# A decoder layer on one core: the feed-forward products cut into 2x2 blocks, seven block products in place of eight

## The chip, the core and the metric

The kernel runs on one core of a Trainium2 chip. A core has a tensor engine (PE in the profile; PEld is its loading of weights), a vector engine (DVE), a scalar engine (ACT), a GpSimd engine (POOL) and a queue that issues most of the transfers (SP). Each engine works through its own queue in order, and waits on semaphores for the others. All data that an engine computes on lies in the on-chip memory of 128 partitions; the tensor engine writes into eight accumulator banks. The metric is the device time of one execution in microseconds (us).

## The reference, cut to what matters

1032 tokens (1024 of a prompt, 8 samples) with 1024 channels go through one decoder layer. In front of the change stand a norm, an input projection, sliding-window attention, a diagonal state-space branch (S5) and a gated merge. The change concerns what follows:

```python
x = x + merged @ w_out                        # 1024 -> 1024
h2 = rms_norm(x, norm2_g)
x = x + (silu(h2 @ w_ffn_gate) * (h2 @ w_ffn_up)) @ w_ffn_down   # 1024 -> 2816 -> 1024
y = rms_norm(x, norm_f_g)
```

with `rms_norm(x, g) = x * rsqrt(mean(x * x) + 1e-5) * g`, all in float32.

## The kernel before

Activations are stored with channels on the 128 partitions and tokens along the free axis: eight tiles of 128 x 1032 make up x. A matrix product goes by output tiles of 128 channels, three chunks of 344 tokens each (`CH`, `NCH`), and input tiles of 128 channels. Float32 is kept by a split: an operand v is written as a high part (v rounded to a shorter format, by ACT) and a low part (v minus the high part, by DVE), and each product is three matmuls: high x high, high x low and low x high (`mm3`, L118 to L120). So one output tile of the gate matrix (`fg`) takes 8 x 3 x 3 = 72 matmuls of 344 columns.

`load_w` brings a weight tile of 128 x 512 from memory (`wr`), splits it (L107 on ACT, L108 on DVE) into `wh` and `wl`, three buffers each, and hands out blocks of 128 columns.

The order of the work that the change touches:

- Output projection (`wo`): for eight output tiles, three chunks; the residual is added (L1001), the result (`mg`, the new x) is multiplied by norm2_g and split (`hh` on ACT L1002, `hl` on DVE L1003), and its squares are summed (`s2`). The norm's factor of each token, `r2`, is ready later; it isn't applied to x but to the products behind it.
- Feed-forward (FFN): 22 output tiles of gate and up, in four parts of 6, 6, 6 and 4 (`FSPLIT`). For each tile: gate product (`fg`), times r2 (L1052), sigmoid (ACT L1053), times itself, times r2 (L1055, L1056); up product (`fu`), times that (L1062), and the result is split into `idh`, `idl`, which stay on chip. After each part its share of the down product (`fd`) is added to x (L1072). The last part runs by blocks of 384, 384 and 264 tokens, and the final norm and the output follow block by block (L1082, L1084, L1141).

The whole body is handed to a scheduler, which puts each engine's instructions in an order of its own before they are placed in the queues; a tile that shares a buffer (tag) with another waits until that one's last reader is done.

## Time and profile before

| | |
|---|---|
| three timed runs | 1456.91 us median (1455.76 to 1459.46) |
| profiled execution, first to last instruction (span) | 1455.0 us |
| PE busy | 1404.8 us (97%) |
| DVE, ACT, POOL busy | 800.7, 458.9, 193.5 us |

The profile gives no other time of the profiled execution than its span, which lies 1.9 us under the median of the timed runs. The stages, read from the tensor engine's timeline: input projection, attention, S5 and merge until 598.3 us; output projection until about 689.5; FFN until 1440.9; norm and output until 1455. A matmul's length in the rows is longer than the time to the next one, since they are pipelined: rates are read from the starts. "idle before ... <-" names what ended an engine's wait.

### The profile page before, as it was taken

Reading aid. Unit: us, or ns where it says so; the run is one execution under the profiler, and the core shown is the slowest. Engines: PE = TensorE matmul, PEld = TensorE weight load, DVE = VectorE, ACT = ScalarE, POOL = GpSimd, SP = SyncE. Lnnn points to the kernel's source line nnn. Section 1 sums busy time; section 2 is a strip of 40 time slices with the busy share of each in tenths; the row PEclk is TensorE's granted clock in tenths of the full one; section 3 lists DMA queues with packets and bytes.
Section 4 is the critical chain, followed back from the end, with each engine's and each line's share of the span. In section 5 each row is a group of like instructions: output and inputs, shape, how many; then the busy total and the mean of one; then the engine's idle time right before and its main releaser. Section 6 shows DMA issues by size and latency. Waiting matters only on the chain.

```text
span 1455.0 us, 22291 instructions
## 1 busy us (share of the span) xinstructions
PE 1404.8 (97%) x8839; PEld 1370.5 (94%) x8839; DVE 800.7 (55%) x1825; ACT 458.9 (32%) x967; POOL 193.5 (13%) x218
## 2 busy tenths in 40 slices
PE   7799999998899999999999999999999999999996
PEld 6689999997788999999999999999999999999996
DVE  4675976269988744655744423444334444335447
ACT  3323655433334623333322211222111222113242
POOL 1113321066673001000000000000000000000004
PEclk9799999999999999999999999999999999999998
DMA  6111100111111111223111111111111111123003
GB/s 230 50 36 61 30 16 16 44 60 46 31 32 39 59 54 31 77 88 96 47 49 44 35 53 58 45 44 40 45 50 56 44 44 45 48 63 94 29 1 117
DMA packets 52393, 78.02 MB, mean 54 GB/s; under 512 B 12090, under 2 KB 24386, under 8 KB 52289
## 3 DMA queue, kind: packets, MB, share of 16 engines
q1 hardware_dynamic: 50960, 73.79, 16.5%
q0 software_dynamic: 640, 2.10, 0.5%
q8 instruction: 69, 1.13, 0.3%
q10 hardware_dynamic: 688, 0.72, 0.1%
q14 instruction: 36, 0.29, 0.1%
HBM read 69.84 MB, written 5.55 MB: 52 GB/s over the span
## 4 chain that ended last, share of the span: by engine, by line
PE 84%; DVE 8%; DMA 3%; issue 3%; SPq 1%; ACT 1%; POOL 0%; DVEq 0%; ACTq 0%; POOLq 0%
PE fg L120 6%; PE fu L120 6%; PE fu L119 6%; PE fg L119 6%; PE fd L118 6%; PE fd L120 6%; PE fd L119 6%; PE fg L118 6%; PE fu L118 6%; PE wo L120 2%; PE wo L118 2%; PE wo L119 2%; DMA xr<-in_xT 2%; PE gs L118 2%; PE gs L120 2%
## 5 line engine op out<-in xcount | busy, mean ns | idle before, releaser
L119 PE MATMUL fg<-hl,wh_fg 128*128 128x344 f32 x528 | 169.0, 320 | 0.0
L118 PE MATMUL fg<-hh,wh_fg 128*128 128x344 f32 x528 | 168.9, 320 | 0.0
L119 PE MATMUL fu<-hl,wh_fu 128*128 128x344 f32 x528 | 168.8, 320 | 0.0
L118 PE MATMUL fu<-hh,wh_fu 128*128 128x344 f32 x528 | 168.3, 319 | 0.0
L120 PE MATMUL fg<-hh,wl_fg 128*128 128x344 f32 x528 | 165.8, 320 | 0.0
L120 PE MATMUL fu<-hh,wl_fu 128*128 128x344 f32 x528 | 165.6, 320 | 0.0
L120 PE MATMUL fd<-idh,wl_fd 128*128 128x344 f32 x432 | 134.6, 319 | 0.0
L118 PE MATMUL fd<-idh,wh_fd 128*128 128x344 f32 x432 | 134.5, 319 | 0.0
L119 PE MATMUL fd<-idl,wh_fd 128*128 128x344 f32 x432 | 134.5, 319 | 0.0
L1082 POOL TENSOR_TENSOR mg<-mg,r3s 128x384 f32<-128x384 f32 x13 | 14.0, 1112 | 850.1 <-DVE r3s L142 850.1
L119 PEld LDWEIGHTS fg<-hl,wh_fg 128*128 128x128 f32 x528 | 99.3, 188 | 0.3
L118 PEld LDWEIGHTS fg<-hh,wh_fg 128*128 128x128 f32 x528 | 99.3, 188 | 0.2
L119 PEld LDWEIGHTS fu<-hl,wh_fu 128*128 128x128 f32 x528 | 99.3, 188 | 0.0
L118 PEld LDWEIGHTS fu<-hh,wh_fu 128*128 128x128 f32 x528 | 99.3, 188 | 0.0
L120 PEld LDWEIGHTS fg<-hh,wl_fg 128*128 128x128 f32 x528 | 98.7, 188 | 0.1
L120 PEld LDWEIGHTS fu<-hh,wl_fu 128*128 128x128 f32 x528 | 98.6, 188 | 0.0
L1072 DVE TENSOR_TENSOR mg<-fd,mg 128x344 f32<-128x344 f32 x72 | 37.2, 516 | 97.8 <-PE fd L120 97.8
L1062 DVE TENSOR_TENSOR ft<-fu,ft 128x344 f32<-128x344 f32 x66 | 34.1, 516 | 92.5 <-PE fu L120 92.5
L1052 DVE TENSOR_TENSOR ft<-fg,r 128x344 f32<-128x344 f32 x66 | 34.0, 516 | 88.7 <-PE fg L120 88.7
L120 PEld LDWEIGHTS fd<-idh,wl_fd 128*128 128x128 f32 x432 | 80.6, 188 | 0.0
L118 PEld LDWEIGHTS fd<-idh,wh_fd 128*128 128x128 f32 x432 | 80.5, 188 | 0.0
L119 PEld LDWEIGHTS fd<-idl,wh_fd 128*128 128x128 f32 x432 | 80.4, 188 | 0.0
(460 smaller groups left out, 3560.9 us busy)
## 6 DMA issues: line engine op xcount, KB each, us to landing
wr_fg<-in_wfg SPq DMA_DIRECT2D x44, 256.0 KB, 2.7
wr_fu<-in_wfu SPq DMA_DIRECT2D x44, 256.0 KB, 2.7
wr_fd<-in_wfd SPq DMA_DIRECT2D x24, 256.0 KB, 2.6
xres<-in_xT SPq DMA_DIRECT2D x24, 172.0 KB, 3.1
wr_ga<-in_wst SPq DMA_DIRECT2D x16, 256.0 KB, 2.8
wr_gs<-in_wst SPq DMA_DIRECT2D x16, 256.0 KB, 2.9
wr_wo<-in_wout SPq DMA_DIRECT2D x16, 256.0 KB, 2.8
xr<-in_xT SPq DMA_DIRECT2D x7, 516.0 KB, 7.7
```

What stands on the lines that cost most here:

```text
L118: TE.matmul(ps, wh, xh[:, cs], start=(k == 0), stop=False)
L119: TE.matmul(ps, wh, xl[:, cs], start=False, stop=False)
L120: TE.matmul(ps, wl, xh[:, cs], start=False, stop=(k == n - 1))
L1052: V.tensor_tensor(t, ps[:, :CH], r2[:, chunk(c)], op=ALU.mult)
L1062: V.tensor_tensor(ts[c], ps[:, :CH], ts[c], op=ALU.mult)
L1072: V.tensor_tensor(X1[m][:, chunk(c)], ps[:, :CH], X1[m][:, chunk(c)], op=ALU.add)
L1082: P.tensor_tensor(y, y, rs, op=ALU.mult)
```

## The change

**Blocks.** The tokens are cut into two stretches of 516 (`SC`, s = 0, 1) and each of these into two halves of 258 (`HC`). A product W x X is cut into 2x2 blocks: two halves of the output channels, two halves of the input channels, two halves of a stretch's tokens. The four block results are put together from seven block products in place of eight. The seven operands on the side of X are sums and differences of its four blocks, made and split by `combine`; those on the side of W are made and split by `seven`: four sums on POOL (s1 to s4), seven splits (ACT, DVE). The seven products run through `products`: product i for both stretches, then the next; each has 4 input tiles x 3 matmuls of 258 columns for each stretch (3 input tiles in the last section of the down product). Results of two products can be added in a bank; four banks for each stretch.

**Around the products.** The output projection stays as it was, but runs stretch by stretch in halves of 258. r2 is now made by columns (`rstd`, `across`), and x is multiplied in place by norm2_g and r2 before the operands `ho` are made (L1127). x before that is put into memory (`x1d`) and read again for the residual. The gate's sigmoid and its products work on 516 columns; the gated activations go to memory (`hid`) by rows of 128, and are read again for the down product (`hr`), which runs in three sections of 4, 4 and 3 pairs of tiles, whose operands `do0`, `do1`, `do2` use the buffers of `ho`, each in the place of the one before. The first two of the eleven gate and up pairs run for stretch 0 alone, and for stretch 1 alone at the end; the last section of the down product runs stretch by stretch as well, and the final norm follows each stretch.

```diff
+    POS = [[f"T{i}" for i in range(4)] + [f"Zl{i}" for i in range(4)] + [f"h{i}" for i in range(6)],
+           [f"A{i}" for i in range(14)]]
+    def combine(ops, k, b, name, engs):
+        t = buf(TSUM[combine.n % 2], f"ts_{name}", F32, (128, 4, HC))
+        combine.n += 1
...
+        e[0].tensor_tensor(t1, b12, b11, op=ALU.subtract)
+        e[1].tensor_tensor(t3, b22, b12, op=ALU.subtract)
+        e[2].tensor_tensor(t2, b22, t1, op=ALU.subtract)
+        e[3].tensor_tensor(t4, b21, t2, op=ALU.subtract)
+        for i, src in enumerate((b11, t1, t3, b21, t2, b22, t4)):
+            hi, lo = (ops[i][j][:, k] for j in range(2))
+            S.copy(hi, src)
+            (P if i in (5, 6) else V).tensor_tensor(lo, src, f32(hi), op=ALU.subtract)
+    def seven(loads, n, name):
...
+        a11 = raw(0)
+        a21, a22 = raw(2), raw(3)
+        yield sp2(0, a11)
+        s1 = sm(1, a21, a22, ALU.add)
+        yield sp2(1, s1)
+        s3 = sm(3, a11, a21, ALU.subtract)
+        yield sp2(2, s3)
+        a12 = raw(1)
+        yield sp2(3, a12)
+        s2_ = sm(2, s1, a11, ALU.subtract)
+        yield sp2(4, s2_)
+        s4 = sm(4, a12, s2_, ALU.subtract)
+        yield sp2(5, s4)
+        yield sp2(6, a22)
+    BANK = (0, 2, 3, 1, 0, 2, 3)
+    def products(weights, ops, stretches, name, after):
+        bank = {}
+        for i, w in enumerate(weights):
+            q, first = BANK[i], i < 4
+            for s in stretches:
...
+                for k, (wh, wl) in enumerate(w):
+                    bh, bl = ops[s][i][0][:, k], ops[s][i][1][:, k]
+                    TE.matmul(ps, wh, bh, start=(first and k == 0), stop=False, skip_group_check=True)
+                    TE.matmul(ps, wh, bl, start=False, stop=False, skip_group_check=True)
+                    TE.matmul(ps, wl, bh, start=False, stop=(k == n - 1), skip_group_check=True)
+                after(i, s, ps)
...
+        for k in range(4):
+            b = []
+            for j in (k, k + 4):
+                t = X1[j][:, stretch(s)]
+                V.scalar_tensor_tensor(t, t, g2[:, j:j + 1], r2[:, stretch(s)], op0=ALU.mult, op1=ALU.mult)
+                b += [X1[j][:, half(s, 0)], X1[j][:, half(s, 1)]]
+            combine(HO[s], k, b, f"h{k}{s}", (V, P))
...
+    NE2 = 2
+    for f in range(NE2):
+        hidden(f, (0,))
+    for f in range(NE2, NP):
+        hidden(f, (0, 1))
+    for f in range(NE2):
+        hidden(f, (1,))
...
+    SECT = ((2, 3, 4, 5), (6, 7, 8, 9), (10, 0, 1))
+    RAWH = ("Zh2", "M6")
...
+    def hid_operands(si, s):
+        ops = operands(s, f"do{si}")
+        for k, f in enumerate(SECT[si]):
+            t = buf(RAWH[nraw[0] % 2], f"hr{si}{s}{k}", F32, (128, 4, HC))
...
+            combine(ops, k, [t[:, i] for i in range(4)], f"d{si}{s}{k}", (P, P))
...
+            elif i == 4:
+                kept["u2", s] = hp.tile([128, HC], F32, tag="hu2", name=f"u2{nm}", bufs=2)
+                S.copy(kept["u2", s], ps)
+                for x in (x22, x12, x21):
+                    P.tensor_tensor(x, x, kept["u2", s], op=ALU.add)
...
+    for si in range(2):
+        DO = [hid_operands(si, s) for s in range(2)]
+        for m in range(4):
+            products(seven(down_rows(m, SECT[si]), 128 * len(SECT[si]), f"d{si}{m}"), DO, (0, 1), f"d{si}{m}",
+                     down_after(m, False))
```

`P` is POOL, `V` DVE, `S` ACT, `TE` PE, `SY` SP. Up to the last 36 matmuls of the merge the order of every engine's instructions is the same in both kernels.

**The order at two places.** POOL, before: the rows behind the end of S5 are the low parts of the merge's result (`ml`), and then at once the final norm.

```order
L857 COPY hfin_521<-H_6_4499 128x4
L846 MEMSET H_7_4653 128x4
L857 COPY hfin_521<-H_7_4653 128x4
L459 TENSOR_TENSOR ml1_6265<-mg1_2429,mh1_6257 128x344 x3
L459 TENSOR_TENSOR ml3_6267<-mg3_2797,mh3_6259 128x344 x3
L1082 TENSOR_TENSOR mg0_2030<-mg0_2030,r3s0_13630 128x384
L1082 TENSOR_TENSOR mg1_2429<-mg1_2429,r3s0_13630 128x384
```

POOL, now, at the turn from the first section of the down product to the second: `do15l` and `do16l` are the low parts of operands 5 and 6 of the second section, `ts_d` the sums t1 to t4, `hr` the activations read from memory, `ws4_d10` a weight sum. The digits behind `hr` and `ts_d` give section, stretch and pair: `hr102` is section 1, stretch 0, pair 2.

```order
L1027 TENSOR_TENSOR do15l0_14789<-hr100_14792,do15h0_14788 128x258
L1027 TENSOR_TENSOR do15l0_14789<-hr101_14814,do15h0_14788 128x258
L1042 TENSOR_TENSOR ws4_d10_15170<-wr1_d10_15096,ws2_d10_15130 128x512
L1027 TENSOR_TENSOR do16l0_14791<-ts_d100_14795,do16h0_14790 128x258
L1027 TENSOR_TENSOR do16l0_14791<-ts_d101_14817,do16h0_14790 128x258
L1042 TENSOR_TENSOR ws1_d11_15274<-wr2_d11_15234,wr3_d11_15236 128x512
L1020 TENSOR_TENSOR ts_d102_14839<-hr102_14836 128x258
L1021 TENSOR_TENSOR ts_d102_14839<-hr102_14836 128x258
L1020 TENSOR_TENSOR ts_d103_14861<-hr103_14858 128x258
L1027 TENSOR_TENSOR do15l0_14789<-hr102_14836,do15h0_14788 128x258
L1021 TENSOR_TENSOR ts_d103_14861<-hr103_14858 128x258
L1027 TENSOR_TENSOR do15l0_14789<-hr103_14858,do15h0_14788 128x258
```

POOL, which before had nothing to do between the merge and the final norm, now stands between two sections with 54 instructions, from the first of these rows to `do16l1` of pair 3. PE goes, behind the last matmul of a section, straight to operands 0, 1 and 2 of the next, as far as the first pairs of stretch 0 reach.

DVE, before, in the output projection: the residual (L1001) and the split of x (L1003) of a tile alternate with the weight splits (L108) of the next.

```order
L108 TENSOR_TENSOR wl_wo1_512_6454<-wr_wo1_512_6451,wh_wo1_512_6453 128x512
L1001 TENSOR_TENSOR mg0_2030<-wo02_6416,xres02_6414 128x344
L108 TENSOR_TENSOR wl_wo2_0_6559<-wr_wo2_0_6556,wh_wo2_0_6558 128x512
L1003 SCALAR_TENSOR_TENSOR hl0_6331<-mg0_2030,vec_62,hh0_6323 128x344
L1001 TENSOR_TENSOR mg1_2429<-wo10_6459,xres10_6457 128x344
L1003 SCALAR_TENSOR_TENSOR hl1_6332<-mg1_2429,vec_62,hh1_6324 128x344
```

DVE, now, behind the output projection of stretch 1, while PE runs the first gate and up pair for stretch 0: the end of eight scalings (L1127), then one weight split (`wl4_u00`) among the operands of stretch 1 (`ho0l1`, `ho2l1`, `ho3l1`).

```order
L1127 SCALAR_TENSOR_TENSOR mg7_2805<-mg7_2805,vec_62,r2_6356 128x516
L1020 TENSOR_TENSOR ts_h01_7711<-mg0_2030 128x258
L1049 TENSOR_TENSOR wl4_u00_8033<-ws2_u00_8030,wh4_u00_8032 128x512
L1027 TENSOR_TENSOR ho0l1_7696<-mg0_2030,ho0h1_7695 128x258
L1027 TENSOR_TENSOR ho3l1_7702<-mg4_2802,ho3h1_7701 128x258
L1020 TENSOR_TENSOR ts_h11_7732<-mg1_2429 128x258
L1027 TENSOR_TENSOR ho0l1_7696<-mg1_2429,ho0h1_7695 128x258
L1027 TENSOR_TENSOR ho2l1_7700<-ts_h01_7711,ho2h1_7699 128x258
L1027 TENSOR_TENSOR ho3l1_7702<-mg5_2803,ho3h1_7701 128x258
L1027 TENSOR_TENSOR ho0l1_7696<-mg2_2796,ho0h1_7695 128x258
```

The operands of a whole stretch, which before were made tile by tile as the output projection went on, now stand in one piece behind it, and the weight splits for PE's next products stand between them: from the first scaling to the first weight split of the second pair (`wl0_g10`) there are 43 instructions, four of them weight splits.

## Rows read from the trace of the kernel before

**Rows 1.** Page of the profile: busy time by engine; 40 slices, busy tenths and granted clock.
```profile
PE 1404.8 (97%) x8839; PEld 1370.5 (94%) x8839; DVE 800.7 (55%) x1825; ACT 458.9 (32%) x967; POOL 193.5 (13%) x218
PE   7799999998899999999999999999999999999996
PEclk9799999999999999999999999999999999999998
```

**Rows 2.** Stretches of the span: busy us (instructions) by engine; PE clock, DMA share, GB/s.
```profile
300.00:400.00 100.00, 86.84 (x538) 79.30 (x537) 92.18 (x185) 33.80 (x71) 69.66 (x73) 0.93 0.16 45
...
1100.00:1200.00 100.00, 100.00 (x637) 100.00 (x636) 45.16 (x83) 23.23 (x43) 0.00 (x0) 1.00 0.15 48
```

**Rows 3.** Timeline of PE (start us, length us): ends of the stage, matmuls of 264 columns.
```profile
598.34 0.32 PE L118 MATMUL wo<-mh,wh_wo 128*128 128x344 f32 x1
...
1435.01 0.28 PE L119 MATMUL fd<-idl,wdh 128*128 128x264 f32 x1
...
1439.89 0.28 PE L120 MATMUL fd<-idh,wdl 128*128 128x264 f32 x1
...
1440.61 0.28 PE L120 MATMUL fd<-idh,wdl 128*128 128x264 f32 x1
```

**Rows 4.** Groups by line, POOL (count | busy us, mean ns): sums in S5, final norm.
```profile
L773 POOL TENSOR_TENSOR INT<-INT,X 128x512 f32<-128x512 f32 x8 | 11.2, 1403 | 0.3
L771 POOL TENSOR_TENSOR INT<-bst,PR 128x512 f32<-128x512 f32 x8 | 9.6, 1198 | 0.7 <-DVE bst L706 0.7
L832 POOL TENSOR_TENSOR TS<-TS,X 128x256 f32<-128x256 f32 x8 | 6.7, 840 | 0.6
L830 POOL TENSOR_TENSOR TS<-UR,TI 128x256 f32<-128x256 f32 x8 | 5.7, 710 | 11.8 <-DVE RE L852 11.8
L1082 POOL TENSOR_TENSOR mg<-mg,r3s 128x384 f32<-128x384 f32 x13 | 14.0, 1112 | 850.1 <-DVE r3s L142 850.1
```

**Rows 5.** Groups by line, DVE and ACT, the same columns.
```profile
L108 DVE TENSOR_TENSOR wl_fd<-wr_fd,wh_fd 128x512 fp32r<-128x512 f32 x24 | 16.6, 692 | 0.8 <-ACT wh_fd L107 0.6
L1092 DVE TENSOR_TENSOR mg<-fd,mg 128x264 f32<-128x264 f32 x8 | 3.3, 429 | 2.0 <-PE fd L120 2.0
L852 DVE TENSOR_TENSOR RE<-RE,TS 128x256 f32<-128x256 f32 x8 | 3.3, 410 | 0.0
L838 DVE TENSOR_TENSOR W<-IM,TC 128x256 f32<-128x256 f32 x8 | 7.6, 948 | 0.2
L839 DVE TENSOR_TENSOR IM<-RE,TS 128x256 f32<-128x256 f32 x8 | 6.5, 811 | 0.1
L107 ACT CAST wh_fd<-wr_fd 128x512 fp32r<-128x512 f32 x24 | 14.9, 621 | 18.7 <-PE fd L119 9.6 <-PE fu L119 3.0 <-PE fg L119 2.6
```

**Rows 6.** Timeline of DVE and POOL in S5 and in the final norm.
```profile
345.96 1.38 POOL L771 TENSOR_TENSOR OUT<-bc,PR 128x576 f32<-128x576 f32 x1
346.36 1.26 DVE L838 TENSOR_TENSOR W<-IM,TC 128x256 f32<-128x256 f32 x1
347.30 1.24 POOL L771 TENSOR_TENSOR INT<-bst,PR 128x512 f32<-128x512 f32 x1
347.65 1.16 DVE L839 TENSOR_TENSOR IM<-RE,TS 128x256 f32<-128x256 f32 x1
353.34 0.68 POOL L830 TENSOR_TENSOR TS<-UR,TI 128x256 f32<-128x256 f32 x1 [3.23 <-DVE RE L852]
360.40 1.05 POOL L772 TENSOR_TENSOR X<-bsw,PI 128x512 f32<-128x512 f32 x1
...
1440.55 5.06 POOL L1082 TENSOR_TENSOR mg<-mg,r3s 128x384 f32<-128x384 f32 x5 [8.76 <-DVE r3s L142]
1443.51 0.17 DVE L129 RECIPROCAL r3t<-r3t 88x3 f32<-88x3 f32 x1 [0.27 <-ACT r3t L128]
1443.72 0.95 DVE L130 TENSOR_TENSOR r3t<-r3t 88x3 f32<-88x3 f32 x1
```

**Rows 7.** Transfers (issue line: count, KB each, median us to landing).
```profile
wr_fd<-in_wfd SPq DMA_DIRECT2D x24, 256.0 KB, 2.6
```

More of the change, by code (lines that the diff above doesn't have):

```diff
@@ L27 @@
 NF = F // 128
-FSPLIT = (6, 6, 6, 4)
+SC = 516
+HC = 258
 NE = 2
@@ new lines, in evh, with half, stretch, operands @@
+    def evh(name):
+        return ev(name)[:, 0:HC]
+    def half(s, q):
+        return slice(SC * s + HC * q, SC * s + HC * q + HC)
+    def stretch(s):
+        return slice(SC * s, SC * s + SC)
+    POS = [[f"T{i}" for i in range(4)] + [f"Zl{i}" for i in range(4)] + [f"h{i}" for i in range(6)],
+           [f"A{i}" for i in range(14)]]
+    def operands(s, name):
+        return [[buf(POS[s][2 * i + e], f"{name}{i}{'hl'[e]}{s}", F32R, (128, 4, HC)) for e in range(2)]
+                for i in range(7)]
@@ new lines, in rows, with load, go, hidden @@
+    def rows(src, f, g, cols):
+        def load(r, a):
+            def go(t):
+                SY.dma_start(t[:, 0:512], src[r][:, a:a + 512])
+            return go
+        return [load(f, 0), load(f, 512), load(g, 0), load(g, 512)]
+    def hidden(f, stretches):
+        for gate in (True, False):
+            src = h["wfg"] if gate else h["wfu"]
+            nm = f"{'ug'[gate]}{f}{stretches[0]}"
+            products(seven(rows(src, f, f + NP, None), 512, nm), HO, stretches, nm, gated(f, None)(gate))
@@ new lines, in body_, with runs @@
+    NE2 = 2
[5 more added lines that the diff above has]
+        hidden(f, (1,))
+    XT = ("A14", "Zh3", "Zh0", "Zh1", "A15", "M7", "M4", "M5")
+    X = [None] * KD
+    for m in (0, 4, 1, 5, 2, 6, 3, 7):
+        X[m] = buf(XT[m], f"x2{m}")
+        SY.dma_start(X[m], x1d[m])
+    SECT = ((2, 3, 4, 5), (6, 7, 8, 9), (10, 0, 1))
+    RAWH = ("Zh2", "M6")
+    TSUM = ("r", "h6")
+    def runs(fs):
+        out = []
+        for f in fs:
+            if out and out[-1][0] + out[-1][1] == f:
+                out[-1][1] += 1
+            else:
+                out.append([f, 1])
+        return out
@@ L1148, in _rope_tables @@
+    h2p.__exit__(None, None, None)
 def _rope_tables():
```

328 lines of the change are left out of this document (178 added, 150 removed).

## The prediction

> **What bounds the kernel now.** I read the page first: PE is busy 97% of the span, with the clock at its upper level except near the start, in S5 and at the end [rows 1]. Then the stretches: behind the merge PE is busy without a gap and starts 637 matmuls in 100 us, 0.157 us each for 344 columns, while DVE is busy 45% and POOL not at all [rows 2]. The stage that the change rewrites runs from the first matmul of the output projection at 598.3 to the end of the last of the FFN at 1440.9 [rows 3]: 842.6 us, all of it PE's. So the rate of PE's starts bounds it now, and every other engine has room. The last view is the timeline of S5, the one place where POOL and DVE are both loaded (70 and 92 us of 100) and PE falls to 87 [rows 2]: that is what the new stage would look like wherever POOL has to keep up.
>
> **PE's own work.** Forty starts in a row of 264 columns take 1439.89 - 1435.01 = 4.88 us, 0.122 each [rows 3]. 264 columns at 2.4 GHz are 0.110, so 0.012 lies on top (344 columns: 0.143 and 0.0135). For 258 columns that gives 0.1195. Now counted: output projection 2 stretches x 8 x 2 x 24 = 768 matmuls (before 576 of 344 columns); gate and up 22 x 7 x 2 x 12 = 3696; down 4 x 7 x 2 x 33 = 1848. Together 6312 x 0.1195 = 754.3 us, and about 7 for the small matmuls of the two norms. Against 842.6 this is 81 us less, not the eighth of the FFN's products alone (some 94), since a shorter matmul keeps its 0.012. If weight loading needed more at 258 columns, 264 would have shown it; I allow 0.122, 16 us more.
>
> **What is added elsewhere.** POOL gets 548 instructions where it had 15, DVE and ACT some 200 and 470 more than before. Prices: POOL 256 columns 0.71 to 0.84, 512 columns 1.20 to 1.40, 384 columns 1.11 [rows 4]; the shortest alone are 0.68 and 1.05 [rows 6]. I take 0.78 for 258, 1.25 for 512 and 516, and as short prices 0.68, 0.87 (384, between the two) and 1.05. DVE 512 columns 0.69 (516: 0.70), 264 from an accumulator 0.43, 256 undisturbed 0.41, and 0.81 to 0.95 where POOL works beside it [rows 5]. The timeline shows how: POOL's sum runs from 345.96 to 347.34, and DVE's, due at 346.36, ends at 347.62, one undisturbed data pass later; the next pair does the same; at the end of the kernel a DVE product of 88x3 that should take 0.17 takes 0.95 beside POOL [rows 6]. DVE with two inputs on chip waits for POOL's instruction to end. I charge 0.4 us for each such DVE instruction.
>
> That is the Trainium skill's rule too ("SBUF — State Buffer", section "Who interferes with whom": the pair of ports that VectorE and GpSimd share is locked for a whole instruction, also against a VectorE instruction with two SBUF inputs; one SBUF input is free of it). The trace agrees; taken to its end, with no overlap of any such pair, it gives the third case below.
>
> **Where it is hidden.** For f = 2 to 10 a gate or up block is 168 matmuls, 20.1 us of PE. POOL has at most 4 x 1.25 + 2 x 0.78 + 4 x 1.25 = 11.6, DVE 7 x 0.69 + 8 x 0.43 + 4 x 0.70 = 11.1 and 11 x 0.4 of waits, ACT about 7 x 0.62 and ten smaller; the weights stay two products (5.7 us) ahead. No stall: 18 blocks at PE's rate. So too the last three blocks of each of the first two down sections. Transfers (512 columns land in 2.6 us [rows 7]) are issued blocks ahead; only `hr`, with two buffers, waits for its last reader.
>
> **Where it isn't.** A stall is the engine's queue between two marks, less PE's work in that time.
> - Operands of stretch 0, under the second output projection: DVE 60 instructions beside 36 us of PE, weights among them. 0 to 6 us; I take 3.
> - Operands of stretch 1. The scalings start about 14 us behind the output projection (101 matmuls and the norm factor's chain). Then 43 DVE instructions: 8 x 0.70 + 4 x 0.69 + 6 x 0.43 + 25 x 0.43 = 21.7, and up to 29 x 0.4 of waits, 33.3. Only then comes the first weight of the second pair. PE has 168 matmuls, 20.1. Stall 16 to 27; 21, since POOL is busy for half of it.
> - The last two pairs for stretch 1 alone: 40 us of PE, DVE 58 instructions, 32.8 and up to 42 x 0.4 = 49.6. 0 to 10; 5.
> - Into the down product. Operands of its first section take the places of the old ones, and only two sets of sums (`ts`) and of raw tiles fit ahead. POOL from the first gate product of the last pair (10 us before PE's end of the up block) to the last low part: 56 instructions, 47 x 0.78 + 9 x 1.25 = 47.9. ACT and the last matmuls add 1.8; less 10, less 20.1 of PE. Stall 20 (13 with the short prices).
> - First to second section: 54 instructions, 50 x 0.78 + 4 x 1.25 = 44.0, begun 4.3 us ahead (36 matmuls), 1.8 behind; PE has 195 matmuls, 23.3. Stall 18 (12).
> - Third section, in blocks of 63 matmuls (504 in all, 60.2 us). POOL: 68 x 0.78 + 29 x 1.11 + 6 x 1.25 = 92.7, with its lead and end about 88. DVE: 126 instructions, 64 undisturbed and 89 x 0.4 of waits, 100. Neither fits under 60. I take 94: stall 34 (13 with the short prices and no waits).
>
> Together 101 us. In these places PE works in bursts, and a clock as in S5 (0.93 [rows 2]) may cost a little: 5. The tail (factor by columns, eight scalings, output) has the form of the old one: no change. Span 1455.0 - 81 + 101 + 5 = 1480; timed, with the 1.9 us by which the median lies above the span, 1482.
>
> **Rivals.**
> 1. Faster: the queues run at the undisturbed prices and DVE finds POOL's gaps. Stalls 16 + 13 + 12 + 13 = 54: 1455 - 81 + 54 = 1428, timed 1430. For it: DVE's data pass is short, and POOL at 0.68 was seen. Against it: S5, where both were loaded, shows the long prices.
> 2. No change: the stalls happen to be near 81. Nothing but the sum speaks for it; 1457.
> 3. Slower by full exclusion: POOL's undisturbed lengths and DVE's data passes (0.27 for 258, 0.40 for 384, 0.53 for 512) simply add. First section 41 + 17.5 (39 DVE instructions of 258, 11 of 512, 2 of 516 columns), stall 31; second 38 + 10, stall 23; third 78 + 35, less the overlaps at its ends, against 60, 48; with 27, 10 and 6 for the others 145. 1455 - 81 + 145 + 5 = 1524, timed 1526. It decides wherever POOL's and DVE's work together exceed PE's.
> 4. Slower by the clock: short blocks with gaps leave PE at 1.2 GHz, where 258 columns take about 0.22. The third section's 504 matmuls then need 111 in place of the 94, and the two turns about 5 more each: 1482 + 27 = 1509. For it: with PE busy 87% the clock is at 0.93 on the mean [rows 2]. Against it: there a few long gaps did it, and the third section's are short.
>
> **Chances.** Forecast 0.38 (its own range 1465 to 1500, from errors of about 15 us in the sum of six stalls), faster 0.25, no change 0.10, full exclusion 0.17, clock 0.10. That gives faster 0.25, same 0.10, slower 0.65, where about 0.3% (4 us) is what a measurement of this kernel tells from no change. The range of 1435 to 1530 leaves out the lower third of the faster case and the upper part of the third and fourth.
>
> **What will show it.** Behind 598 us: PE at 0.12 us a start and without gaps in f = 2 to 10, about 20 us for each block of 168. Gaps of about 20 us at the first pair and at each of the first two turns, PE waiting for operands `ho`, `do0`, `do1` or weights that DVE made late, DVE for POOL. The last section at 90 us or more. POOL near 90% busy there, DVE's 258-column splits at 0.8 us, those from an accumulator at 0.43. Wrong would be: PE busy throughout the turns (case 1), 0.13 us or more a start in the steady blocks (a floor under short matmuls), or a granted clock well under 0.9 at the turns (case 4).

## The result and the profile after

The changed kernel takes 1537.17 us (median of four runs, 1534.63 to 1540.05), the kernel before 1457.03 beside it: ratio 1.0557, 95% interval 1.0536 to 1.0577. The forecast was 1482, in a range of 1435 to 1530: slower was right, the size was not, +80 us for +25. The profiled execution has a span of 1532.9 us, against 1480 forecast: 53 us to be found.

First the page of the profile after, against [rows 1]: busy time of PE and POOL, then PE's busy tenths and its clock in 40 slices of 38 us.

```profile
PE 1390.5 (91%) x9887; PEld 1335.4 (87%) x9887; DVE 1024.0 (67%) x2039; ACT 639.8 (42%) x1432; POOL 756.3 (49%) x751
PE   6799999989889999997599999999998599799785
PEclk9799999999999999999799999999999699699797
```

PE's holes come behind the output projection (the 19th and 20th slice) and again in the last quarter, and the clock falls in most of the same slices. Next the stretches of the rewritten stage, cut at the first matmul of each part (the output projection and the last three blocks of the second section are left out). Columns: stretch and its length, then busy us (instructions) of PE, PEld, DVE, ACT and POOL, PE's clock, DMA share, GB/s; [rows 2] has the same of before.

```profile
701.00:777.70 76.70, 53.42 (x361) 50.21 (x360) 67.55 (x95) 36.63 (x81) 47.02 (x40) 0.82 0.32 101
777.70:1141.00 363.30, 363.30 (x3026) 363.30 (x3025) 189.19 (x310) 135.84 (x270) 179.56 (x146) 1.00 0.25 81
1141.00:1196.50 55.50, 45.83 (x340) 42.95 (x339) 54.69 (x61) 27.83 (x62) 45.73 (x37) 0.97 0.44 140
1196.50:1240.50 44.00, 28.84 (x169) 26.21 (x168) 30.43 (x42) 20.18 (x52) 42.46 (x50) 0.69 0.48 151
1240.50:1301.00 60.50, 60.50 (x506) 60.50 (x505) 36.05 (x58) 23.61 (x53) 47.90 (x54) 1.00 0.19 53
1301.00:1345.20 44.20, 33.31 (x168) 27.56 (x167) 31.53 (x43) 21.12 (x55) 43.51 (x51) 0.69 0.37 116
...
1406.00:1514.00 108.00, 85.11 (x530) 77.50 (x528) 94.92 (x126) 56.90 (x133) 101.39 (x101) 0.84 0.28 85
```

In order: first two pairs, the 18 steady blocks, last two pairs, first block of the down product's first section, its other three, first block of the second section, third section. In the steady blocks PE is busy for the whole 363.3 us, with POOL at 180 and DVE at 189 beside it: no stall. In the two first blocks POOL is busy for 42.5 of 44.0 and 43.5 of 44.2 us, in the third section for 101 of 108. In the first two pairs and the last two it is DVE, 54.7 of 55.5 in the latter.

PE's timeline, against [rows 3] (start, length): two first matmuls of steady blocks, two neighbours in a turn, the last matmul of the stage.

```profile
777.71 0.28 PE L1082 MATMUL g20b<-ho0h,wh_g 128*128 128x258 f32 x1
...
797.86 0.28 PE L1082 MATMUL u20b<-ho0h,wh_u 128*128 128x258 f32 x1
...
1217.94 0.42 PE L1084 MATMUL d00b<-do01h,wl_d 128*128 128x258 f32 x1
1218.16 0.42 PE L1082 MATMUL d00b<-do01h,wh_d 128*128 128x258 f32 x1
...
1513.50 0.28 PE L1084 MATMUL d231b<-do26h,wl_d 128*128 128x258 f32 x1
```

168 matmuls in 20.15 us are 0.1199 each; 0.1195 was forecast. In the turn the starts are 0.215 to 0.22 apart: 258 columns at 1.2 GHz. The stage ends at 1513.50 + 0.28 = 1513.8 and began at 599.0: 914.8 us. Taking 0.12 us for each matmul off every stretch gives the stalls (in the third section for the 504 matmuls of the products, as the forecast did; with the 26 small ones of the final norm of stretch 0 its stall is 44):

| part | forecast | measured |
|---|---|---|
| operands of stretch 0, under the output projection | 3 | 6.5 |
| first two pairs (operands of stretch 1) | 21 | 33 |
| last two pairs | 5 | 15 |
| first block of section 1 | 20 | 24 |
| first block of section 2 | 18 | 24 |
| third section | 34 | 47 |
| clock | 5 | in the above |
| tail (last product to last instruction: 14.1 before, 19.1 after) | 0 | 5 |

Stalls and clock were forecast as 106 us and are 150; with the tail, 3 to 4 us of PE's own time and 0.7 of a later begin that makes the 53.

Now the groups of the third section, against [rows 4] and [rows 5]: POOL first (count | busy us, mean ns | idle before).

```profile
L1266 POOL TENSOR_TENSOR x<-x,u2d 128x258 f32<-128x258 f32 x24 | 19.6, 840 | 1.1 <-ACT u2d L1264 1.1
L1042 POOL TENSOR_TENSOR ws_d<-wr_d,wr_d 128x384 f32<-128x384 f32 x14 | 17.9, 1284 | 0.0
L1042 POOL TENSOR_TENSOR ws_d<-wr_d,ws_d 128x384 f32<-128x384 f32 x8 | 10.0, 1249 | 1.2 <-issue 1.2
L1308 POOL TENSOR_TENSOR x<-x,r 128x516 f32<-128x516 f32 x6 | 9.8, 1672 | 0.0
L1253 POOL TENSOR_TENSOR x<-x,p1d 128x258 f32<-128x258 f32 x8 | 8.1, 1010 | 1.7 <-ACT p1d L1252 1.7
```

DVE in the same stretch:

```profile
L1049 DVE TENSOR_TENSOR wl_d<-ws_d,wh_d 128x384 fp32r<-128x384 f32 x31 | 29.1, 937 | 5.2 <-ACT wh_d L1048 5.0
L1049 DVE TENSOR_TENSOR wl_d<-wr_d,wh_d 128x384 fp32r<-128x384 f32 x23 | 25.0, 1095 | 2.2 <-ACT wh_d L1048 2.2
```

POOL's sums are longer than the prices of the prediction (0.78, 1.11, 1.25), and its idle times are near nothing: its queue is the fullest there, with DVE's (94.9 us busy) close behind. How the two hold each other is seen in the timeline of the last two pairs, against [rows 6]:

```profile
1160.16 1.74 POOL L1042 TENSOR_TENSOR ws_g<-ws_g,wr_g 128x512 f32<-128x512 f32 x1
...
1160.67 1.77 DVE L1049 TENSOR_TENSOR wl_g<-wr_g,wh_g 128x512 fp32r<-128x512 f32 x1
...
1161.86 1.09 POOL L1161 TENSOR_TENSOR cu<-cu,u2u 128x258 f32<-128x258 f32 x1
```

POOL's sum ends at 1161.90; DVE's split, due at 1160.67, ends at 1162.44, 0.54 behind it; POOL's next sum, which takes 0.64 when it is alone, takes 1.09 and ends 0.51 behind DVE's split: it is longer by about DVE's half microsecond. Both sides pay.

The first pair has one more thing. DVE's timeline there:

```profile
713.63 0.42 DVE L1101 TENSOR_TENSOR mg<-wo,xres 128x258 f32<-128x258 f32 x1 [0.20 <-DMA xres<-in_xT]
714.54 0.43 DVE L1107 TENSOR_TENSOR s<-s,sq 128x258 f32<-128x258 f32 x1 [0.49 <-ACT sq L1106]
...
724.92 3.22 DVE L1127 SCALAR_TENSOR_TENSOR mg<-mg,vec,r 128x516 f32<-128x516 f32 x4
```

The last product of the output projection starts at 700.8, but its last residual tile (`xres`) is added only at 713.6, and the scalings of stretch 1 begin at 724.9: 24 us behind, where the prediction had 14.

### The profile page after: what moved, and what is told of

The parts are those of the page before. It is cut to its first block, busy times and chain, and to the rows that moved or that the text cites. A ratio compares the mean times of both kernels' runs of the same rounds, so it can differ in the third digit from the quotient of the medians.

```text
span 1532.9 us, 26607 instructions
## 1 busy us (share of the span) xinstructions
PE 1390.5 (91%) x9887; PEld 1335.4 (87%) x9887; DVE 1024.0 (67%) x2039; ACT 639.8 (42%) x1432; POOL 756.3 (49%) x751
## 4 chain that ended last, share of the span: by engine, by line
PE 68%; DVE 15%; DMA 5%; issue 4%; POOL 3%; ACT 2%; SPq 2%; DVEq 0%; ACTq 0%; POOLq 0%
DVE wl_d L1049 2%; PE gs L119 2%; PE gs L121 2%; PE gs L120 2%; DMA xr<-in_xT 2%; DMA hr<-hid 1%; SPq L102 1%; DMA xres<-in_xT 1%; PE q L120 1%; PE q L119 1%; PE ps L121 1%; PE ps L119 1%; PE q L121 1%; PE ps L120 1%; PE wo L119 1%
## 5 line engine op out<-in xcount | busy, mean ns | idle before, releaser
L119 PE MATMUL wo<-mh,wh_wo 128*128 128x258 f32 x256 | 72.0, 285 | 4.0 <-ACT wh_wo L108 4.0
L121 PE MATMUL wo<-mh,wl_wo 128*128 128x258 f32 x256 | 70.7, 284 | 1.6 <-DVE wl_wo L109 1.6
L120 PE MATMUL wo<-ml,wh_wo 128*128 128x258 f32 x256 | 71.1, 283 | 0.0
L1049 DVE TENSOR_TENSOR wl_d<-ws_d,wh_d 128x512 fp32r<-128x512 f32 (+1 forms) x64 | 59.7, 936 | 15.2 <-ACT wh_d L1048 13.9
L1042 POOL TENSOR_TENSOR ws_u<-wr_u,wr_u 128x512 f32<-128x512 f32 x26 | 37.9, 1459 | 53.6 <-issue 31.2
L1049 DVE TENSOR_TENSOR wl_u<-ws_u,wh_u 128x512 fp32r<-128x512 f32 x52 | 49.9, 960 | 21.1 <-ACT wh_u L1048 17.3
L121 PE MATMUL gs<-xh,wl_gs 128*128 128x344 f32 x192 | 61.8, 322 | 0.0
L119 PE MATMUL gs<-xh,wh_gs 128*128 128x344 f32 x192 | 61.6, 322 | 0.0
L120 PE MATMUL gs<-xl,wh_gs 128*128 128x344 f32 x192 | 61.5, 321 | 0.0
L1266 POOL TENSOR_TENSOR x<-x,u2d 128x258 f32<-128x258 f32 x72 | 55.1, 795 | 8.9 <-ACT u2d L1264 8.9
L1049 DVE TENSOR_TENSOR wl_d<-wr_d,wh_d 128x512 fp32r<-128x512 f32 (+1 forms) x48 | 49.6, 1039 | 13.4 <-ACT wh_d L1048 13.1
L1049 DVE TENSOR_TENSOR wl_g<-ws_g,wh_g 128x512 fp32r<-128x512 f32 x52 | 44.2, 850 | 20.7 <-ACT wh_g L1048 19.8
```

The costliest lines, as they stand in the source:

```text
L119: TE.matmul(ps, wh, xh[:, cs], start=(k == 0), stop=False)
L120: TE.matmul(ps, wh, xl[:, cs], start=False, stop=False)
L121: TE.matmul(ps, wl, xh[:, cs], start=False, stop=(k == n - 1))
L1042: P.tensor_tensor(t, x, y, op=op)
L1049: V.tensor_tensor(wl[:, 0:n], src, f32(wh[:, 0:n]), op=ALU.subtract)
L1266: P.tensor_tensor(x, x, kept["u2", s], op=ALU.add)
```

## The experiments

Four theories stand behind the expectations. A: a DVE instruction with two on-chip inputs and a POOL instruction exclude each other, so that each lengthens the other, and where their work together exceeds PE's, PE waits. B: the prediction's own prices, a fixed length for POOL and 0.4 us of wait on DVE's side alone. C: PE's clock at 1.2 GHz behind the gaps. D: the hidden tiles' transfers, with two raw buffers. A1 and A1' concern the late norm factor of stretch 1. Each kernel is the changed kernel with one edit unless said; "before" ran beside each at 1455 to 1457.

### POOL's work in the down product left out

```diff
         def sm(q, x, y, op):
+            if name[0] == 'd':
+                return x
...
+        if name[0] == 'd':
+            t1, t3, t2, t4 = b12, b22, b12, b21
...
-                P.tensor_tensor(x11, x11, kept["p1", s], op=ALU.add)
```

> In the down product POOL's sums and low parts are left out (operands and weights are formed from the raw tiles, low parts 5 and 6 by DVE, nothing is added to the residual by POOL). Theory A, DVE with two SBUF inputs and POOL exclude each other, so that their lengths add: with POOL gone DVE's 384-column splits fall from 0.94 to 1.08 us to 0.55, its 258-column ones from 0.75 to 0.85 to 0.43; the third section (107.8 us for 60 of PE) falls to 60 to 70, each of the two turns' 24 us of stall to 3 to 8; time about 1537 - 40 - 35 = 1462. Theory C, PE's clock at 1.2 GHz after gaps: about 21 us at these places are half-speed starts and go only if the gaps go. Theory D, the two raw buffers and the 3 us transfers bound the turns: the turns keep at least 15 us each, time 1485 or more.

Measured: 1473.26 us, ratio 1.0111 (1.0089 to 1.0134), so 64 us of the 80 hang on POOL's work there. The two first blocks lose 8 and 12 us, the third section is 75.3 long (A had 3 to 8, and 60 to 70). Its stretch and DVE's splits in it:

```profile
1379.70:1455.00 75.30, 69.47 (x530) 65.42 (x528) 64.05 (x133) 55.49 (x133) 9.50 (x6) 0.98 0.41 128
```
```profile
L1053 DVE TENSOR_TENSOR wl_d<-wr_d,wh_d 128x384 fp32r<-128x384 f32 x54 | 31.7, 599 | 2.3 <-ACT wh_d L1052 2.3
```

The same splits take 0.60 us for 0.94 to 1.10. Theories B and A both say that; C is weakened, since in the third section the clock came back (0.98) with the gaps. The turns keep 8 and 12 us and the section some 15 above PE's 60 without any POOL sum: more than A had, less than D's 15 in the turns. What holds them there is not shown; the run with eight products, which also has four operand splits for seven, is all but without these stalls.

### DVE's splits with one on-chip input

```diff
-            V.tensor_tensor(wl[:, 0:n], src, f32(wh[:, 0:n]), op=ALU.subtract)
+            V.tensor_tensor(wl[:, 0:n], src, junk[:, 0:n] if name[0:2] == 'd2' else f32(wh[:, 0:n]), op=ALU.subtract)
```

> In the third down section DVE's splits (weights and operands) take their second input from an accumulator bank that holds zeros, so that they have one SBUF input; same instructions, columns and order, the low parts are then not the low parts. Theory A: DVE's 384-column splits fall from about 1.0 to 0.55 us and POOL's 384-column sums, which are not touched, from 1.28 to 1.0; the section is then bounded by POOL alone, about 80 us for 107.8, time about 1510. Theory B, POOL keeps its length and only DVE waits (the prices of the prediction): POOL's sums stay at 1.28, the section goes down by 10 at most, time 1527 or more. Theory C (clock): no change beyond the gaps that go.

Measured: 1522.43 us, ratio 1.0460 (1.0445 to 1.0476); section 95.8 us. POOL's groups, whose instructions were not touched, then DVE's:

```profile
L1269 POOL TENSOR_TENSOR x<-x,u2d 128x258 f32<-128x258 f32 x24 | 15.6, 673 | 3.4 <-ACT u2d L1267 3.4
L1045 POOL TENSOR_TENSOR ws_d<-wr_d,ws_d 128x384 f32<-128x384 f32 x8 | 8.1, 1008 | 0.0
L1256 POOL TENSOR_TENSOR x<-x,p1d 128x258 f32<-128x258 f32 x8 | 5.9, 741 | 0.7 <-ACT p1d L1255 0.7
```
```profile
L1052 DVE TENSOR_TENSOR wl_d<-ws_d,junk 128x384 fp32r<-128x384 f32 x32 | 17.5, 550 | 7.0 <-PE d200b L1087 2.1 <-PE d211b L1087 1.3 <-POOL x L1269 0.8
```

POOL's 0.84 fell to 0.67, 1.25 to 1.01, 1.01 to 0.74; DVE's 0.94 to 0.55. That refutes B, in which POOL keeps its length: the exclusion is mutual, and it goes when DVE has one on-chip input. The Trainium skill says so ("SBUF — State Buffer", section "Who interferes with whom": a VectorE instruction with at most one SBUF input, outside its two-port modes, does not contend with GpSimd); this trace agrees, 0.55 us beside a busy POOL. The time fell by 15 only, not 27. DVE's instruction that filled the bank waited for a bank ahead of the operands, and the section's first block lost 18 us where it had lost 5 to 6; the next run is without that.

### The same for the weights alone

```diff
+    for a, b in ((0, 258), (258, 384)):
+        TE.matmul(junk[:, a:b], DO[0][0][0][:, 0, 0:128], DO[0][0][0][:, 0, 0:b - a], start=True, stop=True)
```

> As in the run with the splits from a bank of zeros, but for the weights of the third down section alone: two idle products write the bank before the section's first product, so DVE no longer waits for a bank ahead of the operands (that wait held DVE until 1397 in the earlier run and cost the section's first block 18 us). The weights' low parts are then not the low parts. Theory A: the section falls from 107.8 to 82 to 90 us, POOL's 384-column sums to 1.0 us, time 1512 to 1520. Theory B: POOL's sums stay at 1.28, the section at 98 or more, time 1527 or more.

Measured: 1527.76 us, ratio 1.0486 (1.0467 to 1.0505). The time is B's, POOL's lengths are A's. The section, then two of POOL's groups in it:

```profile
1410.30:1508.10 97.80, 75.12 (x530) 69.23 (x528) 72.47 (x128) 57.54 (x134) 84.62 (x100) 0.93 0.31 97
```
```profile
L1266 POOL TENSOR_TENSOR x<-x,u2d 128x258 f32<-128x258 f32 x24 | 15.8, 684 | 2.0 <-ACT u2d L1264 2.0
L1042 POOL TENSOR_TENSOR ws_d<-wr_d,ws_d 128x384 f32<-128x384 f32 x8 | 8.1, 1014 | 1.2 <-issue 1.2
```

POOL's lengths are as A says, and DVE has room now (72 of 98), yet the section only falls by 10 us: 85 us of POOL's own work and 13 in which its in-order queue waits (6 for ACT, 4 for DVE, 2 for transfers). So the exclusion by the weights' splits is worth some 10 of the 47 us. The run before, which has the operands' splits too, comes to 84 without the 12 us more of its start, but POOL had that time as a lead: 24 us is an upper bound. The amount of POOL's work, 85 us beside 60 of PE, is most of the rest.

### Idle matmuls to keep the clock up

```diff
+                if name[0:2] == 'd2':
+                    for _ in range(4):
+                        TE.matmul(junk[:, 0:HC], w[0][0], ops[s][i][0][:, 0], start=True, stop=True)
```

> In the third down section four idle matmuls of 258 columns into a spare bank follow each group of nine, so that PE has less empty time there (504 matmuls become 728, 87 us at 0.12). Theory C: the 139 starts at 0.215 us go to 0.12, the section loses 13 us or more of 107.8, time about 1524. Theory A: the section is set by DVE and POOL, the half-speed starts lie inside their time; the clock rises but the time moves by less than 4 us.

Measured: 1538.23 us, ratio 1.0567 (1.0547 to 1.0588), as without them. The third section:

```profile
1408.00:1521.50 113.50, 100.89 (x755) 95.71 (x753) 94.21 (x126) 58.14 (x133) 101.26 (x101) 0.95 0.26 82
```

The clock rose from 0.84 to 0.95, POOL and DVE are as busy as before (101.3 and 94.2 for 101.4 and 94.9), and the time did not move. (The section is 113.5 us here for 108.0, but the profiled execution is this kernel's longest of four, 1539.0 us, and that of the changed kernel its shortest, 1532.9.) The idle matmuls are 27 us of PE's work themselves, so a gain at the clock that they took back is not excluded by the time alone; but POOL had only 7 of the 108 us free without them, so most of the half-speed starts lie in time that PE would have waited anyway, and C falls as the cause in the third section. In the two turns it was not tried.

### Additions to the residual from the accumulator

```diff
-                kept["p1", s] = evh(f"p1{nm}")
-                S.copy(kept["p1", s], ps)
-                P.tensor_tensor(x11, x11, kept["p1", s], op=ALU.add)
+                V.tensor_tensor(x11, ps, x11, op=ALU.add)
...
-                for x in (x22, x12, x21):
-                    P.tensor_tensor(x, x, kept["u2", s], op=ALU.add)
+                for x in (x22, x12, x21):
+                    V.tensor_tensor(x, ps, x, op=ALU.add)
```

> In the down product the five additions to the residual that went by an ACT copy and a POOL sum are done by DVE directly from the accumulator (0.43 us each, one SBUF input). Theory A: per block and stretch 5 x 0.64 us of POOL leave the shared time and DVE's additions do not enter it; third section 107.8 to about 84 (DVE passes 34 + POOL 50), each turn about 6 less, time about 1500. Theory B, each queue by itself with 0.4 us of wait per DVE instruction: DVE's queue in the third section grows from 100 to 117, time 1540 to 1550. Theory C: no change beyond the gaps that go.

Measured: 1522.99 us, ratio 1.0466 (1.0449 to 1.0483): faster by 14, so not B, but far from A's 37. The section is 99.7 us:

```profile
1403.50:1503.20 99.70, 79.19 (x530) 72.73 (x528) 95.27 (x165) 50.45 (x109) 62.94 (x60) 0.90 0.28 88
```

DVE, now with 40 more instructions and busy for 95 us, is the engine that has no room, while POOL's 101 us fell to 63. DVE's queue is in order, so an addition that POOL could not hold stands behind a split that it does (those are still 0.84 us long). A sum of locked times alone is too low where one queue holds both kinds.

### Third section for both stretches

```diff
-    for s in range(2):
-        for m in range(4):
-            products(seven(...), DO, (s,), f"d{si}{m}{s}", down_after(m, True))
+    for m in range(4):
+        products(seven(...), DO, (0, 1), f"d{si}{m}", down_after(m, True))
+    for s in range(2):
```

> The third down section is computed for both stretches at a time, its weights are summed and split once, not twice; the norm of stretch 0 then comes at the very end. Theory A: POOL loses 16 sums of 384 columns (1.0 us each), DVE 28 splits (0.40 of pass each): section 107.8 to about 80, tail 19 to about 27: time about 1518. Theory C (clock) and D (transfers of the hidden tiles): at most the turn's own part changes, time above 1530.

Measured: 1517.48 us, ratio 1.0419 (1.0404 to 1.0435), A's number. The section:

```profile
1407.40:1484.90 77.50, 69.78 (x506) 66.28 (x504) 56.68 (x89) 42.02 (x99) 67.48 (x79) 0.87 0.17 51
```

It is 30 us shorter, but 11 of them come back behind it (last product to last instruction 30.3 us for 19.1), where both norms now stand: POOL's final scalings of stretch 0 (`x<-x,r`, 9.8 us) have left the section as well. So summing and splitting the weights twice, for half as many matmuls, is worth the 20 us of the time, not the 30 of the section.

### No pair for one stretch alone

```diff
-    NE2 = 2
+    NE2 = 0
```

> No pair is computed for one stretch alone (NE2 = 0 for 2): the weight work of two pairs is done once, not twice, but nothing stands between the output projection and the operands of stretch 1. Theory A (shared time of DVE and POOL is what bounds single-stretch blocks: 43 us of it for 40 of PE): the 14 us at the last two pairs and part of the 33 at the first go, the wait for stretch 1 (24 us norm factor chain and 17 us of operands) stands alone as about 40: time about 1527. Rival (single-stretch pairs hide the operands of stretch 1 as meant): the stall at the start grows to 55 or more, time 1545 or more.

Measured: 1526.21 us, ratio 1.0480 (1.0465 to 1.0496): A's number. But the parts differ: the start loses 28, the last pairs nothing, and the first block of section 1 now 35 for 24, where no single-stretch pair frees the operand places of stretch 0 early.

### Fetching the residual from another queue

```diff
-                SY.dma_start(xr, h["xT"][m][:, cs])
+                (S if s else SY).dma_start(xr, h["xT"][m][:, cs])
```

> In the second stretch's output projection the residual tiles are fetched from ACT's DMA queue, not from SP's, where the trace shows them behind gate and up weights that wait for a buffer (the last one is issued at 711, 10 us after the last product of the output projection; the scalings of stretch 1 start at 724.9, 24 us behind it, where the prediction had 14). Theory A1, that queue makes the norm factor of stretch 1 late: the scalings start about 10 us earlier, the stall at the first pair falls from 33 to about 23, time about 1527. Rival: the stall is set by DVE's own queue (weights of the first pair and the 43 operand instructions): the scalings start earlier and the time stays within 3 us of 1537.

Measured: 1538.04 us, ratio 1.0558 (1.0540 to 1.0576): no change. The scalings began 29 us behind the output projection, so the edit did not make the fetches earlier and leaves A1 untested; what held them is shown by the next run.

### Buffers of their own for the squares

The residual tiles and the squares of the new x shared five buffers (`ev`); a fetch had to wait until a square was added up.

```diff
-                    sq = evh(f"sq2{m}{s}{q}")
+                    sq = hp.tile([128, HC], F32, tag="hu2", name=f"sq2{m}{s}{q}", bufs=2)
```

> The squares of the residual in the output projection get two buffers of their own; until now they shared five (ev) with the residual tiles, so a residual tile could only be fetched when a square had been added up. Neither ACT's nor POOL's DMA queue made those tiles earlier. Theory A1': these five buffers hold the tiles up; the norm factor's chain of stretch 1 gets 8 to 10 us shorter (scalings at about 715 for 724.9) and the stall at the first pair falls from 33 to about 24, time 1527 to 1530. Rival: DVE's queue (weights of the first pair, then 43 operand instructions beside POOL) sets that stall: 1535 to 1538.

Measured: 1524.27 us, ratio 1.0475 (1.0459 to 1.0490). Last product of the output projection, and first scaling of stretch 1:

```profile
697.51 0.28 PE L121 MATMUL wo<-mh,wl_wo 128*128 128x258 f32 x1
```
```profile
711.90 4.28 DVE L1127 SCALAR_TENSOR_TENSOR mg<-mg,vec,r 128x516 f32<-128x516 f32 x4
```

The chain is 14.4 us, the 14 of the prediction; the output projection ends 3 us earlier, the first two pairs lose 26 for 33. A1' holds. The 5 us above the 21 of the prediction that stay are not the chain's.

### The down product by eight block products

Gate and up keep the seven; the down product's blocks, sections and tiles in memory stay.

```diff
-            products(seven(down_rows(...), ...), DO, (0, 1), f"d{si}{m}", down_after(m, False))
+            products8(four(down_rows(...), ...), DO, (0, 1), f"d{si}{m}", down_after(m, False))
...
+            r, c = q // 2, q % 2
...
+                        bh, bl = ops[s][2 * c + e][0][:, k], ops[s][2 * c + e][1][:, k]
+                        TE.matmul(ps, wh, bh, start=(c == 0 and k == 0), stop=False, skip_group_check=True)
```

> Only the output projection, gate and up keep the change; the down product is done by eight block products (same blocks, same sections, same hidden tiles in DRAM), so it needs no sums: four operands and four splits in place of seven, two products added up in a bank, POOL idle. 2112 matmuls for 1848, 31.7 us more of PE. Theory A: the stalls of the two turns and the third section (24 + 24 + 47) fall to about 15 together; time 1537 + 32 - 80 = 1489. Rival (the spilled tiles and their two buffers make the turns late, not the sums): turns keep 15 us each or more, time 1515 or more.

Measured: 1471.41 us, ratio 1.0106 (1.0087 to 1.0126): 66 us faster with 264 matmuls more. From the down product's first to its last matmul (36 others, of the final norm and of the last pair, among them):

```profile
1190.10:1453.50 263.40, 259.16 (x2148) 258.22 (x2147) 121.38 (x254) 76.70 (x161) 10.76 (x7) 0.99 0.33 100
```

The first blocks lose under 1 and 1.7 us, with the same tiles, buffers and transfers: D falls as a cause by itself. The time is 18 below A's, since the stalls left are about 6 (263.4 less 2148 matmuls at 0.12), not 15, and the last two pairs lose 7 us less too, POOL no longer forming the first section's sums beside them.

### The same with the other edits

On that kernel: all pairs for both stretches (`NE2 = 0`), then the residual fetched by POOL's queue as well, then that with `NE2 = 1`.

> The down product by eight block products and no pair for one stretch alone (NE2 = 0). Theory A: the gains of the two runs add where they do not share a stall: the 7 us at the last two pairs and 5 of the 33 at the first go: 1471 - 12 = 1459. Rival: with the sums gone from the down product the single-stretch pairs no longer cost anything, 1471 to 1474.

Measured: 1471.99 us, ratio 1.0109 (1.0088 to 1.0130): the rival. The first block of section 1 now waits 10 us for its first operand, in one piece, and gives back what the start and the last pairs gained:

```profile
PE d00b L1254 <- ACT do00h L1263: 10.1, 1, 10.1
```

> As the kernel with eight block products in the down product and all pairs for both stretches; the residual tiles of the second stretch are fetched from POOL's DMA queue, so they wait neither behind the weights on SP's queue nor behind ACT's casts. Theory A1: the last residual lands before the output projection's end, the norm factor's chain (18 us from the last product to the first scaling) is 6 to 9 us shorter: 1451 to 1453, below the kernel before. Rival (as on ACT's queue): POOL's own work holds the fetches, no change from 1459.

Measured: 1469.99 us, ratio 1.0102 (1.0085 to 1.0119): the rival again, in that nothing changed (1471.99 without the edit; neither reached the 1459 that both expectations count from).

> The same with one pair for stretch 0 alone and at the end for stretch 1 alone (NE2 = 1). Theory A: 20 us of PE's work stands under the operands of stretch 1, but DVE and POOL share their time for that pair's weights too: within 5 us of the kernel without such pairs, 1450 to 1458. Rival (the work under the wait counts in full): 10 us or more below it.

Measured: 1468.05 us, ratio 1.0085 (1.0062 to 1.0108); 2 us from the kernel without such pairs is as A said, though both stand 10 us or more above the expected times, since the fetches were no earlier. With the squares in their own buffers, `NE2 = 1` and `NE2 = 0` in turn, the residual on SP's queue:

> Eight block products in the down product, one pair for a stretch alone (NE2 = 1), residual from SP's queue, squares in buffers of their own. Theory A1': 8 to 10 us below the kernel without these buffers (1468): 1458 to 1460, the kernel before being 1456. Rival: 1466 to 1470.

Measured: 1456.70 us, ratio 0.9998 (0.9988 to 1.0007): no difference from the kernel before.

> The same with all pairs for both stretches (NE2 = 0). Here nothing but the chain and the operands stands between the output projection and the first pair, so the chain's 8 to 10 us count in full: 1460 to 1463 for 1472. Rival: 1470.

Measured: 1459.39 us, ratio 1.0026 (1.0016 to 1.0037). Against the run with `NE2 = 0` and no such buffers that is 12.6 us, as much as in the changed kernel (12.9). Two more edits on the first of these two, the last scaling by halves from the accumulator and norm2_g multiplied on ACT:

```diff
+                        V.scalar_tensor_tensor(y, y, gf[:, m:m + 1], RP[q][:, 0:HC], op0=ALU.mult, op1=ALU.mult)
...
+            S.activation(t, t, AF.Copy, scale=g2[:, m:m + 1])
```

> The kernel with eight block products in the down product, NE2 = 1 and squares in their own buffers (1456.7), and for stretch 1 the last scaling by halves of 258: DVE takes the norm factor from the accumulator (one SBUF input, so POOL beside it does not hold it), the first half starts before the second half's factor is there. The tail (last product to the last instruction 19 us, 14 in the kernel before) loses about 3 us: 1453 to 1454. Rival: the output transfers end last whatever the scaling does, 1456 to 1457.

Measured: 1454.83 us, ratio 0.9995 (0.9986 to 1.0004). In the profiles the tail is 16.1 us for 18.4, but the time lies between the two forecasts and its ratio can't be told from that of the kernel without the edit.

> The same, and x is multiplied by norm2_g on ACT while the norm factor of the FFN's input is made; DVE then multiplies by the factor alone (0.70 us for 0.95, eight for each stretch). Theory A: 2 us less ahead of the operands of stretch 1: 1451 to 1453. Rival: ACT's eight instructions (0.73 us each) stand ahead of its square root and casts and make the chain later: 1454 to 1460.

Measured: 1459.88 us, ratio 1.0034 (1.0022 to 1.0047): the rival. The eight multiplications on DVE for stretch 1 took 1.07 us each, not 0.70 (with the gain in them it was 1.08 in the run before), and ACT's own waited for the transfers that save x.

### All by seven, with less shared time

Additions from the accumulator, third section for both stretches, squares in their own buffers, in one kernel.

> All products by seven, with the edits that take work from the time DVE and POOL share: additions to the residual from the accumulator (14 us alone), third section for both stretches (20 alone), squares in their own buffers (0 to 10). Theory A: additions and third section cut partly the same time (with both stretches 17 us of stall are left in the third section, nearly all at its start), so less than the sum: 1500 to 1510. Rival, each stall its own cause: the sum, 1493 to 1503 with the buffers and 1503 without.

Measured: 1499.18 us, ratio 1.0296 (1.0281 to 1.0312). The three gains alone were 14.2, 19.7 and 12.9, which would give 1490 if they added; 9 us of them are the same time. My two ranges overlapped, so this says only that, and that seven products in the down product stay some 42 us above eight (1456.70, which has `NE2 = 1` where this has 2).

## Why the prediction came out too low

- **PE's own work**: right. 0.1199 us a start for 0.1195, 18 steady blocks without a stall, also the last three blocks of both sections.
- **Where the stalls are**: right, all six places. What ends them too, in the main: POOL's queue in the turns and the third section, DVE's at the pairs.
- **The step that failed: the prices of POOL and DVE side by side.** I put the exclusion on DVE alone (0.4 us each, which held: 0.94 to 1.10 for 0.55) and gave POOL fixed means from S5 [rows 4]: 0.78, 1.11, 1.25. The second run shows POOL's lengths without the exclusion: about 0.65 to 0.74 for 258 columns, 1.0 for 384; with it the third section has 0.84 to 1.01, 1.25 to 1.28 and 1.67 for 516. [Rows 6] had shown it: the timeline in which DVE waits for POOL also has POOL's sums at 1.24 and 1.05 for the same 512 columns. The third section was forecast at 94 us, from 93 of POOL and 100 of DVE; POOL was busy for 101 of it and the section took 108. Nine of the 14 us are POOL's price; the rest is that POOL stood idle for 7 where a lead of 5 had been taken off. Two queues that both do not fit leave more than the longer one, since each also waits for the other's results. In the turns the price is the smaller part: POOL's 50 and 51 instructions took 42.5 and 43.5 us in the two first blocks, 40.9 and 41.7 at my prices, so 2 us each of the 4 and 6 that I was short; for up to 2 more each see the clock, the rest stays open.
- **The first pair**: 12 us too low. The 14 us for the norm factor's chain counted instructions and left out a buffer: five tiles shared by residual and squares made it 24. With other buffers it is 14.4, and the stall falls by 7. The other 5 would go with the prices: DVE's weight splits there have means of 1.07 to 1.41 us in that run, for 1.09.
- **The last two pairs**: 15 for 5. DVE's splits were priced at 0.69 + 0.4 = 1.09; the trace has means of 1.27 to 1.48 there and single ones of 1.8, as at 1160.67 above, where the wait for a whole POOL sum of 512 columns cost 1.1.
- **The tail**: I said no change, since its form is the old one. It has six sums for three, two halves of the factor through one bank, and 516 columns where the old last block had 264: 19.1 for 14.1. Which of these costs the 5 us is not shown.
- **Clock** (fourth case): the sign that I had set for it was there, a granted clock well under 0.9 at the turns: 0.69 in both first blocks. In the third section (0.84) the half-speed starts cost little, by the run with idle matmuls and POOL's 7 free microseconds. In the turns no run tried it, but the trace gives an estimate. PE's last wait in each, then its first start at full rate again:

```profile
1225.41 0.58 PE L1082 MATMUL d00b<-do03h,wh_d 128*128 128x258 f32 x1 [0.49 <-ACT wh_d L1048]
...
1229.84 0.29 PE L1084 MATMUL d00b<-do03h,wl_d 128*128 128x258 f32 x1
...
1331.56 0.58 PE L1084 MATMUL d10b<-do13h,wl_d 128*128 128x258 f32 x1 [0.20 <-DVE wl_d L1049]
...
1335.60 0.29 PE L1083 MATMUL d10b<-do13l,wh_d 128*128 128x258 f32 x1
```

Between them lie 20 and 18 starts without a wait, in 4.43 and 4.04 us; at 0.12 they take 2.4 and 2.2. So up to 2 us of each turn are the clock's: the 5 that I had put in was near, the 5 for each turn and 17 for the third section of the fourth case were not.
- **Rivals**: the third, full exclusion, with 31, 23 and 48 us for turns and section (24, 24, 47 measured) and 145 in all (150), was the nearest; 1526 leaves out the tail and part of the first pair. That its sum comes so near is in part luck: it has 7 us too much in the first turn and 12 too little at the pairs and under the output projection. It had 0.17. The choice between it and mine was the choice of a price from two rows of S5 means, where the timeline of the same stretch already showed both engines paying.

What the change gains is PE's: some 77 us, 81 forecast. Where it went is shown by the run with eight products in the down product: there the sums, with the splits and additions that go with them, cost 89 us of stall (95, of which 6 stay) for 32 of PE's time saved. In gate and up the seven products do pay for themselves in the steady blocks: by count, 3696 matmuls at 0.12 us for 3168 at 0.157 are 54 us less (no run has gate and up by eight in the same blocks). Where that is spent is seen in the profile of the run at 1456.70 us, gate and up first, then the down product:

```profile
697.60:1171.40 473.80, 454.55 (x3712) 451.67 (x3711) 277.19 (x441) 190.29 (x395) 243.98 (x197) 0.97 0.26 89
1171.40:1437.00 265.60, 260.12 (x2148) 258.67 (x2147) 123.05 (x258) 77.18 (x162) 9.62 (x7) 0.99 0.33 102
```

Less 0.12 us for each matmul these leave 28 us, nearly all at the first pair and the last, and 8; the tail is 4 longer than before. With the edit to the tail the best version ends at 0.9995 of the kernel before. None of the versions beats it by more than can be measured.

## What to carry to other kernels

Fewer products for more sums is a trade between engines: add up the sums' time on DVE and POOL as one resource wherever both have on-chip inputs, stage by stage, and compare it with PE's time of that stage as a first estimate (where one in-order queue holds both kinds of work, as with the additions from the accumulator, it is too low); average room says nothing about the places where operands change. A scheme that needs prepared weights wants them used for all tokens at once: halving the matmuls per prepared weight in one section cost 20 us of the time. And before pricing a chain by its instructions, count the buffers that its transfers wait for.

## What the runs showed of the hardware

Exclusion is not a strict turn about. In the run with splits from a bank, one DVE sum with two on-chip inputs stood for 4.63 us while POOL went through five instructions back to back (DVE, then the first and the last two of POOL's):

```profile
1480.23 4.63 DVE L1282 TENSOR_TENSOR s<-s,sq 128x516 f32<-128x516 f32 x1
```
```profile
1480.48 0.99 POOL L1045 TENSOR_TENSOR ws_d<-ws_d,wr_d 128x384 f32<-128x384 f32 x1
...
1482.73 0.63 POOL L1260 TENSOR_TENSOR x<-x,p5d 128x258 f32<-128x258 f32 x1
1483.32 0.98 POOL L1045 TENSOR_TENSOR ws_d<-wr_d,ws_d 128x384 f32<-128x384 f32 x1
```

It ended at 1484.86, 0.56 us behind the last of them. Whether a DVE instruction that waits can be passed over for long in other mixes was not tried.
